# Moving parts of the float32r products at other byte offsets behind the weights, and a norm scratch of two lasting halves

## The chip, the cores and the metric

The kernel runs on one core of one Trainium2 chip. The metric is device time in microseconds, the median of the runs. The profile is of one further execution, taken by the hardware profiler. TensorE is called PE in its rows (PEld for its weight loads), VectorE DVE, ScalarE ACT, GpSimd POOL and SyncE SP.

## The reference

Two layers of a diffusion backbone over 256 latent tokens and 256 context tokens, width 1024, all in float32. Each layer is a feed-forward half block, a mixing stage with four branches, and a second feed-forward half block:

```python
for l in range(DEPTH):
    with_ctx_out = l < DEPTH - 1
    mod = jnp.split(jax.nn.silu(c) @ w_ada[l] + b_ada[l], N_MOD, axis=-1)     # likewise mod_c from c_ctx
    x = ffn_half(x, mod[0], mod[1], mod[2], ffn1_norm[l], ffn1_w_gate[l], ffn1_w_up[l], ffn1_w_down[l])
    h = ffn_half(h, mod_c[0], ...)                                            # the context tokens
    xn, hn = modulate(rmsnorm(x, mix_norm[l]), ...), modulate(rmsnorm(h, mix_norm[l]), ...)
    y, y_c = token_mixing(xn, hn, w_in[l], ..., w_branch[l], w_out[l], rope, with_ctx_out)
    x = x + mod[5] * y
    x = ffn_half(x, mod[6], mod[7], mod[8], ffn2_norm[l], ...)
    if with_ctx_out:
        h = h + mod_c[5] * y_c
        h = ffn_half(h, mod_c[6], mod_c[7], mod_c[8], ffn2_norm[l], ...)
return rmsnorm(x, final_norm)

def swiglu(z, wg, wu, wd):                 # in ffn_half, on the modulated norm of z
    return (jax.nn.silu(z @ wg) * (z @ wu)) @ wd
```

In the last layer the context tokens are needed only as keys and values, so behind its projections it works on 256 tokens, and all before that works on 512.

## The kernel before

**Products.** Features lie on the partitions and tokens along the free dimension, 512 columns for both kinds of tokens (the constant `TT`), 256 for the latent ones alone (`T`). Every large product is made of float32r products of split numbers: a weight is split into whi and wlo, a moving part into a high and a low half, and `mm3` issues three matmuls for each block of 128 features: whi with the high half (line 110), whi with the low half (line 111), wlo with the high half (line 112). Each matmul loads its 128 columns of weights, 512 bytes a partition, and streams 2048 bytes (512 columns) or 1024 bytes (256 columns) of the moving part.

**Stages.** For each layer: `ffn` (pg and pu are the gate and up products, with xs as the moving part; pd and last the down product, with hh and hl), `mix` (proj, gate and the other projections with xs; pb with bh and bl, the split branch outputs; po and last with mh and ml), `ffn` again. An `ffn` runs over two halves of 11 chunks; `first_units` does the first two chunks in blocks of 256 columns, in the very first block `cold_units` does them while the adaptive gains are still being computed (the cold start, up to 66.1 us). While it runs, `ada` sums the gains for later on VectorE and hands each set to PE in eight short matmuls (line 290). The second `ffn` of layer 1 works on 256 columns.

**Weights.** `unit` loads a weight tile (SP's queue), splits it on ScalarE (line 81) and VectorE (line 84), with four buffers of each, so that the tiles stand ready before PE needs them.

**Places.** xs is one long tile; `place` cuts xh and xl, the high and the low half of the normed input, out of it at offsets from the table `PLACES`. `hidden` cuts hh and hl out of padded tiles in the same way. Worked out from the sizes of the tiles in the order of their allocation, in bytes mod 512 (the weight tiles lie at 0; only those few that come from a feed-forward block's own pool lie at 256):

| moving parts | columns | before | after the change |
|---|---|---|---|
| xh, xl in layer 0 and the first `ffn` of layer 1 | 512 | 240, 368 | 368, 496 |
| hh, hl there | 512 | 112, 240 | 112, 496 |
| bh, bl in layer 0 | 512 | 0, 0 | 112, 240 or 368, 496 (two buffers) |
| mh, ml in layer 0 | 512 | 0, 0 | 0, 0 |
| xh, xl in the mixing stage and the second `ffn` of layer 1 | 256 (some 512) | 192, 192 | 448, 448 |
| hh, hl in the second `ffn` of layer 1 | 256 | 192, 192 | 448, 448 |
| bh, bl and mh, ml in layer 1 | 256 | 448, 448 | 448, 448 |

With the change the weights of the blocks' own pools lie at 0 as well, since the tile of hh grows by 256 bytes.

**The norm scratch.** `apply` makes the normed input of one segment (256 columns) for a list of blocks k: VectorE writes nt (line 368), ScalarE makes the high half of xs from it (line 371), VectorE the low half (line 372). nt is a tile of 512 columns with one buffer; each pair of blocks takes a new one and uses its two halves in turn. `cold_units` calls `apply` for a single k at a time, so there each call takes a new tile and uses its first half. The squares of `consts` (line 174) use the same buffer, and so does one tile of `score_parts` in the mixing stage.

**Order.** The order of the instructions on each engine is made by a planner that places every instruction when its operands and its buffer come free in its own model of the costs, earlier ones of the program first.

Of the kernel before, what the change touches and what calls it, by code (L numbers as in the profile page):

```python
# [10 lines left out]
F32 = mybir.dt.float32  # L11
F32R = mybir.dt.float32r
# [5 lines left out]
P = 128  # L18
L = 2
D = 1024  # L20
NK = D // P
T = 256
TT = 2 * T
# [22 lines left out]
LINE = 32  # L46


PLACES = {(0, C_N1): (28, NK * TT + LINE, (28, 12)), (0, C_NM): (28, NK * TT + LINE, None),
          (0, C_N2): (28, NK * TT + LINE, (28, 12)), (1, C_N1): (28, NK * TT + LINE, (28, 12)),  # L50
          (1, C_NM): (16, NK * TT + TT, None), (1, C_N2): (16, NK * TT + TT, (48, 0))}


def ada_chunks(s):
# [4 lines left out]
class Net:  # L59
# [76 lines left out]
    def consts(self):  # L136
        nc, cp, i = self.nc, self.cp, self.i
        self.x = cp.tile([P, NK, TT], F32, name="x")
        self.xs = cp.tile([P, 2 * NK * TT + TT + LINE], F32R, name="xs")
        self.cv = cp.tile([P, NK, 2], F32, name="cv")  # L140
        self.cols = [cp.tile([P, C_END], F32, name=f"cols{l}") for l in range(L)]
        self.mats = cp.tile([P, 3, P], F32, name="mats")
        self.ident, self.perm, self.bones = (self.mats[:, j] for j in range(3))
        for k in range(0, NK, 2):
            nc.sync.dma_start(self.x[:, k:k + 2], i["xT"][:, k:k + 2])
            if k == 0:
                nc.sync.dma_start(self.cv, i["cv"])
        nc.sync.dma_start(self.cols[0], i["cols"][0])
        self.eps = cp.tile([P, 1], F32, name="eps")
        nc.vector.memset(self.eps, EPS)  # L150
        self.junk = cp.tile([P, 1], F32, name="junk")
        self.warm(AF.Silu, self.eps)
        self.ones = cp.tile([P, P], F32, name="ones")
        nc.vector.memset(self.ones, 1.0)

        self.sil = cp.tile([P, NK, 32], F32, name="sil")
        nc.gpsimd.memset(self.sil, 0.0)
        nc.scalar.activation(self.sil[:, :, 0:2], self.cv, AF.Silu)

        self.pick = cp.tile([P, 32], F32, name="pick")  # L160
        nc.gpsimd.memset(self.pick, 0.0)
        for r in range(2):
            nc.gpsimd.memset(self.pick[64 * r:64 * r + 64, r:r + 1], 1.0)
        self.mod = [cp.tile([P, 72, 2], F32, name=f"mod{l}") for l in range(L)]
        self.have = [set() for _ in range(L)]

        ps = [self.aux("stat")[:, :T] for _ in range(2)]
        for k in range(NK):
            for r in range(2):
                sq = self.tp.tile([P, TT], F32, tag="nt", bufs=1, name="sq")[:, :T] if r else self.tp.tile(  # L170
                    [P, T], F32, tag="sq", name="sq")
                x = self.x[:, k, r * T:(r + 1) * T]
                if r:
                    nc.vector.tensor_tensor(out=sq, in0=x, in1=x, op=ALU.mult)
                else:
                    nc.scalar.activation(sq, x, AF.Square)
                nc.tensor.matmul(ps[r], self.ones, sq, start=k == 0, stop=k == NK - 1)
        self.rstd = {r: self.tp.tile([P, T], F32, tag="rstd", name="rstd") for r in range(2)}
        for r in range(2):
            nc.scalar.activation(self.rstd[r], ps[r], AF.Sqrt, scale=1.0 / D, bias=self.eps)  # L180
            nc.vector.reciprocal(self.rstd[r], self.rstd[r])

    def place(self, l, phase):

        h, d, o = PLACES[l, phase]
        self.xh, self.xl = (self.xs[:, a:a + NK * TT].rearrange("p (k t) -> p k t", t=TT) for a in (h, h + d))
        return o

    def keep_warm(self, n):

# [169 lines left out]
    def apply(self, g, sh, r, ks=range(NK)):  # L360

        nc = self.nc
        c0, c1 = HALF[r]
        for j, k in enumerate(ks):
            if j % 2 == 0:
                pair = self.tp.tile([P, TT], F32, tag="nt", bufs=1, name="nt")
            t = pair[:, j % 2 * T:j % 2 * T + T]
            nc.vector.scalar_tensor_tensor(out=t, in0=self.x[:, k, c0:c1], scalar=g[:, k, r:r + 1], in1=self.rstd[r],
                                           op0=ALU.mult, op1=ALU.mult)
            hi = self.xh[:, k, c0:c1]  # L370
            nc.scalar.activation(hi, t, AF.Identity, bias=sh[:, k, r:r + 1])
            nc.vector.scalar_tensor_tensor(out=self.xl[:, k, c0:c1], in0=t, scalar=sh[:, k, r:r + 1],
                                           in1=hi.bitcast(F32), op0=ALU.add, op1=ALU.subtract)
# [88 lines left out]
    def hidden(self, hp, off):  # L462

        return tuple(hp.tile([P, FH * TT + pad], F32R, tag=t, name=t)[:, a:a + FH * TT].rearrange(
            "p (f t) -> p f t", t=TT) for t, pad, a in zip(("hh", "hl"), (48, 16), off))

    def cold_units(self, wgu, hp, evac, off):

# [191 lines left out]
    def score_parts(self, pool, q, k, n, ks=None):  # L660


        nc = self.nc
        qs = [pool.tile([P, TT], F32R, tag=f"qs{h}", name="qs") for h in range(2)]
        ql = [pool.tile([P, TT], F32R, tag="ql", name="ql"), self.tp.tile([P, TT], F32R, tag="nt", bufs=1, name="ql")]
        for h in range(2):
            nc.gpsimd.memset(ql[h][64 - 64 * h:128 - 64 * h, :n].bitcast(F32), 0.0)
        new = ks is None
        if new:
            ks = [pool.tile([P, TT], F32R, tag=f"ks{h}", name="ks") for h in range(2)]  # L670
        for h in range(2):
            own, other = slice(64 * h, 64 * h + 64), slice(64 - 64 * h, 128 - 64 * h)
            nc.scalar.copy(qs[h][own, :n], q[own, :n])
            if new:
                nc.scalar.copy(ks[h][own], k[own])
            nc.scalar.copy(qs[h][other, :n], q[own, :n])
            if new:
                nc.vector.tensor_tensor(out=ks[h][other], in0=k[own], in1=ks[h][own].bitcast(F32), op=ALU.subtract)
            nc.vector.tensor_tensor(out=ql[h][own, :n], in0=q[own, :n], in1=qs[h][own, :n].bitcast(F32), op=ALU.subtract)
        return qs, ql, ks  # L680
# [156 lines left out]
    def mix(self, l, segs):  # L837
# [1 line left out]
        n = T * len(segs)  # L839
        ns = len(segs)  # L840
        cols = self.cols[l]
        self.place(l, C_NM)
        with tc.tile_pool(name=f"mix{l}", bufs=1) as mp:
            acc = mp.tile([P, NK, TT], F32, tag="macc", name="macc")
            if l == 0:
# [2 lines left out]
            def tmp(name, shape=(P, TT)):  # L848
                return bp.tile(list(shape), F32, tag="t", bufs=5, name=name)

            def branch():
                return (mp.tile([P, 2, TT], F32R, tag="bh", bufs=2, name="bh"),
                        mp.tile([P, 2, TT], F32R, tag="bl", bufs=2, name="bl"))

            def merge(b, bo, first=False):

# [388 lines left out]
```

## Time and profile before

| | us |
|---|---|
| median of 3 runs (2144.76 to 2150.27) | 2145.19 |
| the profiled execution | 2152.58 |
| its span, from the first to the last instruction | 2150.8 |
| PE busy in it | 2117.5 |
| DVE busy | 1440.8 |
| ACT busy | 904.6 |
| mean granted clock of PE, share of full | 0.996 |

The profiled execution is 0.3% longer than the median of the runs. "Busy" of PE covers overlapping matmuls: a row's duration runs from its start to its modelled end, and the next matmul starts before that end. The distance of two starts is what one of them costs in a stream.

### The profile page before, as it was taken

Reading aid. Unit: us, or ns where it says so; the run is one execution under the profiler, and the core shown is the slowest. Engines: PE = TensorE matmul, PEld = TensorE weight load, DVE = VectorE, ACT = ScalarE, POOL = GpSimd, SP = SyncE. Lnnn points to the kernel's source line nnn. Section 1 sums busy time; section 2 is a strip of 40 time slices with the busy share of each in tenths; the row PEclk is TensorE's granted clock in tenths of the full one; section 3 lists DMA queues with packets and bytes.
Section 4 is the critical chain, followed back from the end, with each engine's and each line's share of the span. In section 5 each row is a group of like instructions: output and inputs, shape, how many; then the busy total and the mean of one; then the engine's idle time right before and its main releaser. Section 6 shows DMA issues by size and latency. Waiting matters only on the chain.

```text
span 2150.8 us, 31652 instructions
## 1 busy us (share of the span) xinstructions
PE 2117.5 (98%) x12446; PEld 1809.5 (84%) x12446; DVE 1440.8 (67%) x2355; ACT 904.6 (42%) x1488; POOL 39.5 (2%) x95
## 2 busy tenths in 40 slices
PE   7999999999999999999999999999999999999998
PEld 5778778988888888888887888888789989999998
DVE  5987987676366455675676567657665867677555
ACT  3332333456546533433233243323234665656443
POOL 0000000001000000000000000000000000000000
PEclk9999999999999999999999999999999999999999
DMA  7645654321122122343454334445433232355553
GB/s 289 200 166 171 217 185 145 120 77 59 59 89 79 64 88 98 108 148 133 140 179 146 126 129 152 138 142 176 153 119 120 96 118 105 133 180 186 174 194 115
DMA packets 89509, 296.71 MB, mean 138 GB/s; under 512 B 10256, under 2 KB 12176, under 8 KB 89360
## 3 DMA queue, kind: packets, MB, share of 16 engines
q1 hardware_dynamic: 89360, 294.69, 40.7%
q8 instruction: 98, 1.61, 0.3%
q14 instruction: 51, 0.42, 0.1%
HBM read 293.60 MB, written 1.05 MB: 137 GB/s over the span
## 4 chain that ended last, share of the span: by engine, by line
PE 94%; DVE 3%; ACT 2%; issue 1%; DMA 0%; DVEq 0%; ACTq 0%; SPq 0%
PE pg L110 6%; PE pu L110 6%; PE pu L112 6%; PE pg L112 6%; PE pu L111 6%; PE pg L111 6%; PE pd L110 6%; PE pd L112 6%; PE pd L111 6%; PE gate L110 4%; PE gate L112 4%; PE gate L111 4%; PE proj L110 2%; PE proj L111 2%; PE proj L112 2%; PE blev L771 2%
## 5 line engine op out<-in xcount | busy, mean ns | idle before, releaser
L81 ACT CAST whi<-raw 128x1024 fp32r<-128x1024 f32 (+2 forms) x444 | 430.2, 971 | 881.6 <-PE pu L111 213.2
L84 DVE TENSOR_TENSOR wlo<-raw,whi 128x1024 fp32r<-128x1024 f32 (+2 forms) x444 | 498.5, 1124 | 311.4 <-ACT whi L81 308.5
L278 DVE SCALAR_TENSOR_TENSOR aacc<-araw,sil,aacc 128x512 f32<-128x512 f32 x448 | 313.1, 746 | 101.3 <-DMA araw<-in_wada 100.9
L110 PE MATMUL pg<-xs,whi 128*128 128x512 f32 (+1 forms) x640 | 238.0, 372 | 0.8 <-DVE sg L456 0.8
L110 PE MATMUL pu<-xs,whi 128*128 128x512 f32 (+1 forms) x640 | 237.9, 372 | 0.0
L111 PE MATMUL pu<-xs,whi 128*128 128x512 f32 (+1 forms) x640 | 235.1, 367 | 0.0
L111 PE MATMUL pg<-xs,whi 128*128 128x512 f32 (+1 forms) x640 | 235.1, 367 | 0.0
L112 PE MATMUL pg<-xs,wlo 128*128 128x512 f32 (+1 forms) x640 | 234.8, 367 | 0.0
L112 PE MATMUL pu<-xs,wlo 128*128 128x512 f32 (+1 forms) x640 | 234.8, 367 | 0.0
L112 PE MATMUL pd<-hh,wlo 128*128 128x512 f32 (+1 forms) x616 | 224.3, 364 | 0.0
L110 PE MATMUL pd<-hh,whi 128*128 128x512 f32 (+1 forms) x616 | 223.8, 363 | 0.0
L111 PE MATMUL pd<-hl,whi 128*128 128x512 f32 (+1 forms) x616 | 222.8, 362 | 0.0
L110 PE MATMUL gate<-xs,whi 128*128 128x512 f32 (+1 forms) x512 | 175.0, 342 | 0.0
L112 PE MATMUL gate<-xs,wlo 128*128 128x512 f32 (+1 forms) x512 | 173.0, 338 | 0.0
L111 PE MATMUL gate<-xs,whi 128*128 128x512 f32 (+1 forms) x512 | 172.2, 336 | 0.0
L110 PEld LDWEIGHTS pg<-xs,whi 128*128 128x128 f32 x640 | 120.9, 189 | 23.4 <-issue 2.0
L112 PEld LDWEIGHTS pu<-xs,wlo 128*128 128x128 f32 x640 | 121.4, 190 | 22.2
L112 PEld LDWEIGHTS pg<-xs,wlo 128*128 128x128 f32 x640 | 121.4, 190 | 22.2
L110 PEld LDWEIGHTS pu<-xs,whi 128*128 128x128 f32 x640 | 120.9, 189 | 22.3 <-issue 2.0
L111 PEld LDWEIGHTS pu<-xs,whi 128*128 128x128 f32 x640 | 121.2, 189 | 21.0
L111 PEld LDWEIGHTS pg<-xs,whi 128*128 128x128 f32 x640 | 121.2, 189 | 20.8
L110 PEld LDWEIGHTS pd<-hh,whi 128*128 128x128 f32 x616 | 116.3, 189 | 19.5 <-issue 2.2
(276 smaller groups left out, 3809.0 us busy)
## 6 DMA issues: line engine op xcount, KB each, us to landing
raw<-in_wgu SPq DMA_DIRECT2D x176, 512.0 KB, 3.4
araw<-in_wada SPq DMA_DIRECT2D x128, 512.0 KB, 3.2
raw<-in_wgate SPq DMA_DIRECT2D x64, 512.0 KB, 3.2
raw<-in_wd SPq DMA_DIRECT2D x64, 384.0 KB, 3.1
raw<-in_win SPq DMA_DIRECT2D x44, 512.0 KB, 3.2
raw<-in_wd SPq DMA_DIRECT2D x64, 320.0 KB, 2.8
aspace<-in_wada SPq DMA_DIRECT2D x16, 512.0 KB, 9.1
raw<-in_wbr SPq DMA_DIRECT2D x16, 512.0 KB, 3.4
```

The source lines that it names most:

```text
L81: nc.scalar.copy(hi, src)
L84: nc.vector.tensor_tensor(out=lo, in0=src, in1=hi.bitcast(F32), op=ALU.subtract)
L110: nc.tensor.matmul(ps, wh, a, start=first and j == 0, stop=False)
L111: nc.tensor.matmul(ps, wh, b, start=False, stop=False)
L112: nc.tensor.matmul(ps, wl, a, start=False, stop=last and j == n - 1)
L278: nc.vector.scalar_tensor_tensor(out=acc[r], in0=w[:, j], scalar=c, in1=acc[r], op0=ALU.mult, op1=ALU.add)
L771: nc.tensor.matmul(ps[:, g * P:(g + 1) * P], k[:, h, g * P:(g + 1) * P], x[:, h, (g ^ cross) * P:((g ^ cross) + 1) * P], start=True, stop= ...
```

## The change

xs gets 1536 bytes shorter (a multiple of 512, so that what lies behind it keeps its place mod 512), and `PLACES` gets other offsets for it; the tile of hh gets 256 bytes of padding more; the tiles of bh and bl are padded by 256 bytes each and cut at offsets that `PLACES` now gives for the mixing stage, one pair for each of the two buffers. `half` returns the two halves of one lasting nt tile in turn; the squares of `consts` and `apply` take their scratch from it, and `score_parts`, which allocates the same buffer for itself, makes it forget the tile.

```diff
--- before.py
+++ after.py
@@ -46,9 +46,9 @@
 LINE = 32
 
 
-PLACES = {(0, C_N1): (28, NK * TT + LINE, (28, 12)), (0, C_NM): (28, NK * TT + LINE, None),
-          (0, C_N2): (28, NK * TT + LINE, (28, 12)), (1, C_N1): (28, NK * TT + LINE, (28, 12)),
-          (1, C_NM): (16, NK * TT + TT, None), (1, C_N2): (16, NK * TT + TT, (48, 0))}
+PLACES = {(0, C_N1): (60, NK * TT + LINE, (28, 12)), (0, C_NM): (60, NK * TT + LINE, ((28, 60), (28, 60))),
+          (0, C_N2): (60, NK * TT + LINE, (28, 12)), (1, C_N1): (60, NK * TT + LINE, (28, 12)),
+          (1, C_NM): (80, NK * TT, ((0, 0), (64, 64))), (1, C_N2): (80, NK * TT, (112, 0))}
 
 
 def ada_chunks(s):
@@ -136,7 +136,8 @@
     def consts(self):
         nc, cp, i = self.nc, self.cp, self.i
         self.x = cp.tile([P, NK, TT], F32, name="x")
-        self.xs = cp.tile([P, 2 * NK * TT + TT + LINE], F32R, name="xs")
+        self.xs = cp.tile([P, 2 * NK * TT + 5 * LINE], F32R, name="xs")
+        self.nt = None
         self.cv = cp.tile([P, NK, 2], F32, name="cv")
         self.cols = [cp.tile([P, C_END], F32, name=f"cols{l}") for l in range(L)]
         self.mats = cp.tile([P, 3, P], F32, name="mats")
@@ -167,8 +168,7 @@
         ps = [self.aux("stat")[:, :T] for _ in range(2)]
         for k in range(NK):
             for r in range(2):
-                sq = self.tp.tile([P, TT], F32, tag="nt", bufs=1, name="sq")[:, :T] if r else self.tp.tile(
-                    [P, T], F32, tag="sq", name="sq")
+                sq = self.half() if r else self.tp.tile([P, T], F32, tag="sq", name="sq")
                 x = self.x[:, k, r * T:(r + 1) * T]
                 if r:
                     nc.vector.tensor_tensor(out=sq, in0=x, in1=x, op=ALU.mult)
@@ -185,6 +185,13 @@
         h, d, o = PLACES[l, phase]
         self.xh, self.xl = (self.xs[:, a:a + NK * TT].rearrange("p (k t) -> p k t", t=TT) for a in (h, h + d))
         return o
+
+    def half(self):
+
+        if self.nt is None:
+            self.nt, self.nth = self.tp.tile([P, TT], F32, tag="nt", bufs=1, name="nt"), T
+        self.nth = T - self.nth
+        return self.nt[:, self.nth:self.nth + T]
 
     def keep_warm(self, n):
 
@@ -361,10 +368,8 @@
 
         nc = self.nc
         c0, c1 = HALF[r]
-        for j, k in enumerate(ks):
-            if j % 2 == 0:
-                pair = self.tp.tile([P, TT], F32, tag="nt", bufs=1, name="nt")
-            t = pair[:, j % 2 * T:j % 2 * T + T]
+        for k in ks:
+            t = self.half()
             nc.vector.scalar_tensor_tensor(out=t, in0=self.x[:, k, c0:c1], scalar=g[:, k, r:r + 1], in1=self.rstd[r],
                                            op0=ALU.mult, op1=ALU.mult)
             hi = self.xh[:, k, c0:c1]
@@ -462,7 +467,7 @@
     def hidden(self, hp, off):
 
         return tuple(hp.tile([P, FH * TT + pad], F32R, tag=t, name=t)[:, a:a + FH * TT].rearrange(
-            "p (f t) -> p f t", t=TT) for t, pad, a in zip(("hh", "hl"), (48, 16), off))
+            "p (f t) -> p f t", t=TT) for t, pad, a in zip(("hh", "hl"), (112, 16), off))
 
     def cold_units(self, wgu, hp, evac, off):
 
@@ -663,6 +668,7 @@
         nc = self.nc
         qs = [pool.tile([P, TT], F32R, tag=f"qs{h}", name="qs") for h in range(2)]
         ql = [pool.tile([P, TT], F32R, tag="ql", name="ql"), self.tp.tile([P, TT], F32R, tag="nt", bufs=1, name="ql")]
+        self.nt = None
         for h in range(2):
             nc.gpsimd.memset(ql[h][64 - 64 * h:128 - 64 * h, :n].bitcast(F32), 0.0)
         new = ks is None
@@ -839,7 +845,7 @@
         n = T * len(segs)
         ns = len(segs)
         cols = self.cols[l]
-        self.place(l, C_NM)
+        off = self.place(l, C_NM)
         with tc.tile_pool(name=f"mix{l}", bufs=1) as mp:
             acc = mp.tile([P, NK, TT], F32, tag="macc", name="macc")
             if l == 0:
@@ -848,9 +854,13 @@
             def tmp(name, shape=(P, TT)):
                 return bp.tile(list(shape), F32, tag="t", bufs=5, name=name)
 
+            turn = 1
+
             def branch():
-                return (mp.tile([P, 2, TT], F32R, tag="bh", bufs=2, name="bh"),
-                        mp.tile([P, 2, TT], F32R, tag="bl", bufs=2, name="bl"))
+                nonlocal turn
+                turn = 1 - turn
+                pair = [mp.tile([P, 2 * TT + 2 * LINE], F32R, tag=t, bufs=2, name=t) for t in ("bh", "bl")]
+                return tuple(t[:, a:a + 2 * TT].rearrange("p (c t) -> p c t", t=TT) for t, a in zip(pair, off[turn]))
 
             def merge(b, bo, first=False):
```

## Rows read from the trace of the kernel before

**Rows 1.** The page: busy time of each engine, and the chain by engine.

```profile
PE 2117.5 (98%) x12446; PEld 1809.5 (84%) x12446; DVE 1440.8 (67%) x2355; ACT 904.6 (42%) x1488; POOL 39.5 (2%) x95
...
PE 94%; DVE 3%; ACT 2%; issue 1%; DMA 0%; DVEq 0%; ACTq 0%; SPq 0%
```

**Rows 2.** Groups by line and shape, PE: busy us, mean ns of one.

```profile
L110 PE MATMUL pg<-xs,whi 128*128 128x512 f32 x480 | 192.9, 402 | 0.0
...
L111 PE MATMUL pg<-xs,whi 128*128 128x512 f32 x480 | 190.1, 396 | 0.0
L112 PE MATMUL pg<-xs,wlo 128*128 128x512 f32 x480 | 189.9, 396 | 0.0
...
L112 PE MATMUL pd<-hh,wlo 128*128 128x512 f32 x462 | 181.0, 392 | 0.0
L110 PE MATMUL pd<-hh,whi 128*128 128x512 f32 x462 | 180.5, 391 | 0.0
L111 PE MATMUL pd<-hl,whi 128*128 128x512 f32 x462 | 179.5, 389 | 0.0
```

**Rows 3.** Timeline of PE, pg: start us, us, instruction; 17 rows lie between.

```profile
100.86 0.40 PE L110 MATMUL pg<-xs,whi 128*128 128x512 f32 x1
...
105.08 0.40 PE L110 MATMUL pg<-xs,whi 128*128 128x512 f32 x1
```

**Rows 4.** Timeline of PE, pd; 59 rows lie between.

```profile
184.85 0.39 PE L110 MATMUL pd<-hh,whi 128*128 128x512 f32 x1
...
198.45 0.39 PE L110 MATMUL pd<-hh,whi 128*128 128x512 f32 x1
```

**Rows 5.** Timeline of PE, gate and pb: 23 rows lie between, then 5.

```profile
812.74 0.40 PE L110 MATMUL gate<-xs,whi 128*128 128x512 f32 x1
...
818.29 0.39 PE L110 MATMUL pb<-bh,whi 128*128 128x512 f32 x1
...
819.65 0.40 PE L110 MATMUL gate<-xs,whi 128*128 128x512 f32 x1
```

**Rows 6.** Timeline of PE behind the cold units: 16 triples, then 7.

```profile
66.11 0.40 PE L110 MATMUL pg<-xs,whi 128*128 128x512 f32 x1
...
77.20 0.40 PE L110 MATMUL pg<-xs,whi 128*128 128x512 f32 x1
...
82.06 0.40 PE L110 MATMUL pg<-xs,whi 128*128 128x512 f32 x1
```

**Rows 7.** Timeline of PE, layer 1, 256 columns, gate: six triples, then two.

```profile
1722.17 0.28 PE L110 MATMUL gate<-xs,whi 128*128 128x256 f32 x1
...
1724.21 0.28 PE L110 MATMUL pb<-bh,whi 128*128 128x256 f32 x1
...
1724.89 1.05 PE L771 MATMUL blev<-bqz,bk 128*128 128x128 f32 x8
```

**Rows 8.** Timeline of PE, layer 1, last block: eight triples, then eight.

```profile
1967.66 0.28 PE L110 MATMUL pu<-xs,whi 128*128 128x256 f32 x1
...
1970.49 0.28 PE L110 MATMUL pg<-xs,whi 128*128 128x256 f32 x1
...
1973.31 0.28 PE L110 MATMUL pu<-xs,whi 128*128 128x256 f32 x1
```

**Rows 9.** The cold start: PE's waits, timeline, and one stretch by engine.

```profile
PE mm L123 <- ACT xs L371: 8.2, 3, 5.1
...
53.66 0.48 DVE L368 SCALAR_TENSOR_TENSOR nt<-x,gain,rstd 128x256 f32<-128x256 f32 x1
...
56.91 0.48 DVE L368 SCALAR_TENSOR_TENSOR nt<-x,gain,rstd 128x256 f32<-128x256 f32 x1
...
57.98 0.79 PE L123 MATMUL mm<-xs,whi 128*128 128x512 f32 x1 [5.14 <-ACT xs L371]
...
57.00:66.10 9.10, 8.12 (x24) 6.44 (x25) 8.94 (x16) 4.13 (x7) 0.00 (x0) 0.65 0.50 167
```

**Rows 10.** Stretches by engine: length, PE, PEld, DVE, ACT, POOL busy, clock, DMA.

```profile
66.10:169.00 102.90, 102.90 (x464) 81.85 (x463) 86.97 (x132) 35.34 (x48) 0.00 (x0) 1.00 0.54 181
```

## The prediction

> **What bounds the kernel now.** I read the page first: TensorE is busy for 98% of the span, and 94% of the chain of work that ended last is TensorE [rows 1]. Then the groups by line with their shapes, and then the timeline of TensorE alone, because "busy" there says little: the matmuls overlap, so what counts is the distance from one start to the next. Each product of this kernel is a triple on lines 110, 111 and 112 (high weights with high moving part, high weights with low moving part, low weights with high moving part), so I take the distance from one L110 row to the next as the price of a triple. Nothing waits in these stretches; the triples run back to back, and yet they don't all cost the same:
>
> - pg of the first feed-forward block, 512 columns: six triples in 105.08 - 100.86 = 4.22 us, 0.703 us each [rows 3].
> - pd of the same block, 512 columns, same kind of weights, same function: twenty triples in 198.45 - 184.85 = 13.60 us, 0.680 us each [rows 4].
> - gate and pb in a stretch of the mixing stage without side work, 512 columns: eight gate triples in 5.55 us, 0.694 each, and the two pb triples right behind them in 1.36 us, 0.680 each [rows 5].
>
> The last one is the telling one. gate and pb alternate in one stream on one engine, through the same function, with the same weight tiles; what differs is where the moving parts lie (240 and 368 bytes behind the weights, mod 512, for gate; 0 and 0 for pb). pd has 112 and 240. So a triple of 512 columns has at least two prices, 0.680 and about 0.70, and the place of the moving part goes with them. The means of one matmul say the same: 402 + 396 + 396 = 1194 ns for pg and 391 + 389 + 392 = 1172 ns for pd, 22 ns a triple [rows 2].
>
> **The change part by part.**
>
> *xh and xl for 512 columns.* Their places go from (240, 368) to (368, 496), all mod 512; mod 256 that is from (240, 112) to (112, 240), which is where pd has its parts. Does a place count mod 256 or mod 512? In the first chunk behind the cold units the weights come from the block's own pool and lie at 256, so that xh and xl are at (496, 112) there; the chunk behind it has (240, 368). The sixteen triples of the first take 77.20 - 66.11 = 11.09 us, 0.693 each, and seven of the second take 4.86 us, 0.694 each [rows 6]. A shift by 256 changes nothing measurable, so I take (368, 496) as equal to (112, 240), and the price as pd's.
> The three feed-forward blocks that run 512 columns have 20 chunks with 8 triples of pg and 8 of pu in each, 3 x 20 x 16 = 960 triples. I take the 22 ns of the means [rows 2] and not the 23 ns of the undisturbed stretches [rows 3, 4], since the means hold the interruptions by the ada matmuls: 960 x 22 ns = 21.1 us. gate in layer 0 has 4 x 8 x 8 = 256 triples, proj with 512 columns in layer 0 has 15 x 8 = 120. Both are broken up by side work, so I take only the quiet difference of 13.5 ns [rows 5]: 376 x 13.5 ns = 5.1 us. Sum 26.2 us. All of it lies on TensorE, which sets the end; bounds: nothing, if the price goes with something else than the place, and 1336 x 23 ns = 30.7 us, if every triple gains the full step.
>
> *hh, hl, bh, bl.* hh and hl keep (112, 240) mod 256: the tile of hh grows by 256 bytes, so hl and the pool's own weights move by 256, and the weights there come to lie at 0 like all others. bh and bl go from (0, 0) to (112, 240), from 0.680 [rows 5] to 0.680 [rows 4]: nothing. mh and ml stay.
>
> *256 columns, layer 1.* xs and hh/hl go from 192 to 448. Here too there are two prices: 0.340 us a triple (six gate triples in 2.04 us) and 0.353 (eight pu triples in 2.83 us) [rows 7, 8]. But place does not tell them apart. gate at 192 runs at 0.340 and pb at 448 right behind it too, (1724.89 - 1724.21) / 2 = 0.340 [rows 7]; pu at 448 (weights of the block's pool, at 256) runs at 0.353 and pg at 192 right behind it too, 2.82 us for eight [rows 8]. A stream keeps the price with which it began. So I take nothing for this part. Its bounds: the 496 triples of the second feed-forward block (pg 160, pu 160, pd 154, last 22) and the gate and proj triples (328) could all fall to the low price, 824 x 13.3 ns = 11.0 us less, though part of gate is there already [rows 7]; or gate and proj could all go to the high one, at most 328 x 13.3 ns = 4.4 us more.
>
> *The norm scratch.* Until now a call of apply for one k takes a new nt tile with one buffer, so the next call can't write until both readers of the last one are done. With two halves of a lasting tile it can write while ScalarE still reads. The place where this binds is the cold start, where apply is called for single k: TensorE waited there three times, 8.2 us in all, for ScalarE's xs, once for 5.1 us [rows 9]. In that case the nt of the first half ran at 53.66, 0.48 long, and that of the other half only at 56.91, 2.8 us later than it could; the matmul that needs both began at 57.98. The order on VectorE is the planner's, and once the second nt is free to run it should stand right behind the first. I take 2.8 us for this wait, 1.2 us for the two smaller ones, 4.0 us together. [...] The work that nt overtakes (a wlo, an aacc) belongs to weights that are used only behind 66.1, so it costs nothing.
>
> *What is late next.* With TensorE 3% faster in the feed-forward blocks VectorE must keep up: it is busy for 86.97 of 102.90 us in the densest stretch, with the ada sums in it [rows 10]; 22 ns on 1194 make that 85% to 86%. It stays hidden.
>
> [...]
>
> **How the numbers follow.** Sum: 26.2 + 4.0 = 30.2 us. The durations are of the profiled execution, 2152.6 us with a span of 2150.8; the median of the runs is 2145.2, 0.3% below. The steps are steps of a locked stream, so I take them off the median as they are: 2145.2 - 30.2 = 2115.
>
> **The rivals.**
> - *B, layer 1 falls to the low price as well.* For it: which price a stream keeps is settled where it begins, and all beginnings move; against it: 448 shows both prices. If the second feed-forward block goes over as one stream, 496 x 13.3 ns = 6.6 us, and some of gate with it, 2 us: 2106. Chance 0.30.
> - *C, the place is worth nothing* or the change misses its place, and only the scratch counts: the price would go with, say, the PSUM bank or the side engines' work. For it: pg and pd differ in more than the place. Against it: gate and pb [rows 5]. 2145.2 - 4.0 = 2141. Chance 0.08.
> - *D, slower.* Places count mod 512 after all, and (368, 496) is worse than what is there. The place is every 512-column triple on xs: if all of them settle at 0.71 us (an estimate, a little above the 0.703 of [rows 3]), the 960 lose 7 ns (6.7 us) and the 376 lose 16 ns (6.0 us); with the 4.4 us of layer 1 that is 17 us, less the 4.0 of the scratch: 2158. It decides for slower from about 0.705 us a triple on. Against it: [rows 6]. Chance 0.04.
> - *E, half.* xs settles between 0.680 and 0.694, because the last steps of the lock depend on more than the two places: about 13 us less, 2128. Chance 0.08.
> The forecast itself, A, has 0.50.
>
> The range: A's own terms reach from 2145.2 - 30.7 - 10.7 = 2104 to 2145.2 - 21.1 + 4.4 = 2128. B lies in it but for its lower part; with B I let it begin at 2101. E's middle is its upper end. Left out are C, D and the outer parts of B and E, together about 0.2. A measurement of this kernel can tell about 0.3% from no change, 6.4 us: A, B and E are faster by more (0.88), C lies within (0.08), D is slower (0.04).
>
> **What would show each step.** Right, if L110 rows of pg and gate with 512 columns come 0.680 us apart, the mean of the three pg rows falls from 1194 to about 1172 ns, and those of pd stay; wrong, if pg stays at 0.70. The scratch: TensorE's wait for xs on L123 falls from 8.2 to about 4 us, with nt rows in pairs before 66 us, and the first pg row comes 4 us earlier than 66.11. Layer 1: pg and pu of the last block still 0.353 us a triple; 0.340 is B. What would make it all wrong: a plan that sets the work of the mixing stage in another order, with new waits there; idle time of TensorE in that stage would show it.

## The result, and the profile after

The kernel after takes 2115.5 us (median of 2109.65, 2115.50, 2115.57 and 2115.61), the kernel before 2147.7 us in the runs beside it (2144.76 to 2151.32). The ratio is 0.984, with an interval of 0.982 to 0.987. The profiled execution of after took 2115.61 us with a span of 2113.8 us; that of before took 2152.58 us with 2150.8 us.

One thing has to be known to read any of these times. The runs of nearly every kernel here fall into two groups some 6 us apart: before at 2143 to 2147 and 2150 to 2153, after near 2109.6 and near 2115.5. It is one stretch that makes them, the second feed-forward block of layer 1, the last block of the kernel, whose 496 triples of 256 columns run at 0.340 us each in some executions and at 0.353 in others. 496 x 13.3 ns = 6.6 us. In the eight profiled executions of kernels whose runs fall into two such groups, price and group go together every time. Both profiled executions, of before and of after, are of the upper group, so they can be compared as they stand; of the medians, after's lies in the upper group, before's 2147.7 between the two, and the 2145.2 from which the prediction started in the lower one.

The page of after: busy time by engine, and the chain that ended last, by engine. TensorE is still 94% of that chain [rows 1].

```profile
PE 2087.5 (99%) x12446; PEld 1801.0 (85%) x12446; DVE 1434.9 (68%) x2355; ACT 904.5 (43%) x1488; POOL 39.4 (2%) x95
...
PE 94%; DVE 2%; ACT 2%; issue 1%; DMA 0%; DVEq 0%; ACTq 0%; SPq 0%
```

The groups by line and shape of after, TensorE (busy us, mean ns of one). The three matmuls of a pg triple have gone from 402 + 396 + 396 to 391 + 388 + 392 ns; those of pd stand where they were [rows 2].

```profile
L112 PE MATMUL pg<-xs,wlo 128*128 128x512 f32 x480 | 188.1, 392 | 0.0
L110 PE MATMUL pg<-xs,whi 128*128 128x512 f32 x480 | 187.5, 391 | 0.0
L111 PE MATMUL pg<-xs,whi 128*128 128x512 f32 x480 | 186.4, 388 | 0.0
L112 PE MATMUL pd<-hh,wlo 128*128 128x512 f32 x462 | 181.0, 392 | 0.0
L110 PE MATMUL pd<-hh,whi 128*128 128x512 f32 x462 | 180.5, 391 | 0.0
L111 PE MATMUL pd<-hl,whi 128*128 128x512 f32 x462 | 179.4, 388 | 0.0
```

The timeline of after, start and length in us. First VectorE in the cold start: nt now comes in pairs, where before its two halves lay 3.25 us apart [rows 9]. Then the first pg triple behind the cold units, then seven triples of pg, and at the end the last block.

```profile
47.58 0.88 DVE L373 SCALAR_TENSOR_TENSOR nt<-x,gain,rstd 128x256 f32<-128x256 f32 x2
50.31 0.87 DVE L373 SCALAR_TENSOR_TENSOR nt<-x,gain,rstd 128x256 f32<-128x256 f32 x2
...
55.00 0.39 PE L110 MATMUL pg<-xs,whi 128*128 128x512 f32 x1
...
88.28 0.39 PE L110 MATMUL pg<-xs,whi 128*128 128x512 f32 x1
...
93.04 0.39 PE L110 MATMUL pg<-xs,whi 128*128 128x512 f32 x1
...
1927.28 0.36 PE L110 MATMUL pg<-xs,whi 128*128 128x256 f32 x1 [0.44 <-ACT xs L376]
...
1935.83 0.28 PE L110 MATMUL pu<-xs,whi 128*128 128x256 f32 x1
...
1938.66 0.28 PE L110 MATMUL pg<-xs,whi 128*128 128x256 f32 x1
...
1941.49 0.28 PE L110 MATMUL pu<-xs,whi 128*128 128x256 f32 x1
```

Seven pg triples take 93.04 - 88.28 = 4.76 us, 0.680 each, against 0.703 before [rows 3]. The first pg row comes at 55.00 and not at 66.11 [rows 6]. In the last block eight pu triples take 2.83 us and the eight pg triples behind them too: 0.353, as before [rows 8].

The waits of TensorE in the first 70 us, and the stretch ahead of the first pg row (length, then busy time of PE, PEld, DVE, ACT and POOL, granted clock, DMA share, GB/s). Where before lost 8.2 us to three waits for xs and ran the stretch behind the longest of them at a clock of 0.65 [rows 9], after loses 2.6 us, and the stretch ahead of its first pg row is at 1.00.

```profile
PE mm L123 <- ACT xs L376: 2.6, 3, 0.9
```

```profile
49.00:55.00 6.00, 5.91 (x25) 4.51 (x25) 6.00 (x12) 4.23 (x7) 0.00 (x0) 1.00 0.25 87
```

So the two profiled executions divide cleanly at the first pg row. Up to it: 66.11 - 55.00 = 11.1 us gained. From it to the end: (2150.8 - 66.1) - (2113.8 - 55.0) = 25.9 us. Together 37.0 us (group against group the runs give 35; the profiled execution of before lies at the top of its group). The prediction had 4.0 and 26.2.

### The profile page after: what moved, and what is told of

It reads as the page before. It is cut to its first block, busy times and chain, and to the rows that moved or that the text cites. A ratio compares the mean times of both kernels' runs of the same rounds, so it can differ in the third digit from the quotient of the medians.

```text
span 2113.8 us, 31650 instructions
## 1 busy us (share of the span) xinstructions
PE 2087.5 (99%) x12446; PEld 1801.0 (85%) x12446; DVE 1434.9 (68%) x2355; ACT 904.5 (43%) x1488; POOL 39.4 (2%) x95
## 4 chain that ended last, share of the span: by engine, by line
PE 94%; DVE 2%; ACT 2%; issue 1%; DMA 0%; DVEq 0%; ACTq 0%; SPq 0%
PE pg L110 6%; PE pu L110 6%; PE pg L112 6%; PE pu L112 6%; PE pg L111 6%; PE pu L111 6%; PE pd L110 6%; PE pd L112 6%; PE pd L111 6%; PE gate L112 4%; PE gate L110 4%; PE gate L111 4%; PE proj L111 2%; PE proj L110 2%; PE proj L112 2%; PE blev L777 2%
## 5 line engine op out<-in xcount | busy, mean ns | idle before, releaser
L110 PE MATMUL pg<-xs,whi 128*128 128x512 f32 (+1 forms) x640 | 232.5, 363 | 0.4 <-ACT xs L376 0.4
L110 PE MATMUL pu<-xs,whi 128*128 128x512 f32 (+1 forms) x640 | 232.3, 363 | 0.0
L111 PE MATMUL pg<-xs,whi 128*128 128x512 f32 (+1 forms) x640 | 231.4, 362 | 0.0
L111 PE MATMUL pu<-xs,whi 128*128 128x512 f32 (+1 forms) x640 | 231.3, 361 | 0.0
L110 PE MATMUL pd<-hh,whi 128*128 128x512 f32 (+1 forms) x616 | 223.8, 363 | 0.0
L110 PE MATMUL gate<-xs,whi 128*128 128x512 f32 (+1 forms) x512 | 172.5, 337 | 0.0
L110 PEld LDWEIGHTS pg<-xs,whi 128*128 128x128 f32 x640 | 120.8, 189 | 20.8 <-issue 1.8
L110 PEld LDWEIGHTS pu<-xs,whi 128*128 128x128 f32 x640 | 120.8, 189 | 20.1 <-issue 2.0
L111 PEld LDWEIGHTS pu<-xs,whi 128*128 128x128 f32 x640 | 120.2, 188 | 19.4
L111 PEld LDWEIGHTS pg<-xs,whi 128*128 128x128 f32 x640 | 120.2, 188 | 19.4
L110 PEld LDWEIGHTS pd<-hh,whi 128*128 128x128 f32 x616 | 116.2, 189 | 19.5 <-issue 2.2
```

The source lines that it names most:

```text
L110: nc.tensor.matmul(ps, wh, a, start=first and j == 0, stop=False)
L111: nc.tensor.matmul(ps, wh, b, start=False, stop=False)
```

## The experiments

Two theories were to be told apart first. **The place theory**, that of the prediction: a triple's price goes with where its two moving parts lie relative to the weights, mod 256. **The rival**: the price goes with something else that pd has and pg has not, and most of the gain comes from the cold start. After the first runs a second question was added: what sets the price of the last block.

### The place alone

```
 (the change, but in consts and apply the scratch as before:)
-            t = self.half()
+            if j % 2 == 0:
+                pair = self.tp.tile([P, TT], F32, tag="nt", bufs=1, name="nt")
+            t = pair[:, j % 2 * T:j % 2 * T + T]
...
```

> The new places with the norm scratch of before. Theory 1 (places and scratch are two separate gains, places as in the sum, scratch larger than the sum said): 25 to 26 us less than before, pg triples of 512 columns at 0.680 us, first pg row still near 66.1 us. Theory 2 (the places gained more than the trace of after shows, through what comes later): 30 us less or more. Theory 3 (they help each other, the places alone are worth less): 20 us less or fewer.

Measured: 2120.4 us (2119.5 to 2121.0), ratio 0.988 (0.986 to 0.990). Its last block runs at 0.340, so it stands beside the lower group of before (2143.8 to 2145.9 in these runs): 24.5 us. Its first pg row comes at 66.16, as before. Groups of this run by line and shape; 277 and 276 ns are a block at 0.340; before and after, profiled at 0.353, have 281 to 282 ns in these rows:

```profile
L110 PE MATMUL pg<-xs,whi 128*128 128x256 f32 x160 | 44.2, 277 | 0.8 <-DVE sg L464 0.8
L110 PE MATMUL pu<-xs,whi 128*128 128x256 f32 x160 | 44.2, 276 | 0.0
```

Added up over the timeline, from each L110 row to the next, the triples of pg and pu with 512 columns are 19.4 us shorter in the kernel after than in the one before (716 to 695 ns on average, interruptions included), those of gate 3.9 us and those of proj 1.9 us: 25.2 us, within 1 us of what this run shows.

### The scratch alone

```
 (the kernel before, with the scratch of the change:)
-            t = pair[:, j % 2 * T:j % 2 * T + T]
+            t = self.half()
...
-                sq = self.tp.tile([P, TT], F32, tag="nt", bufs=1, name="sq")[:, :T] if r else ...
+                sq = self.half() if r else ...
```

> The places of before with the two lasting halves. Theory 1: 10 to 11 us less than before, first pg row near 55 us, TensorE's wait for xs on L123 near 2.6 us and no half clock between 46 and 66 us. Theory of the sum on record: 4 us less, first pg row near 62 us. Theory 3: nearly nothing, since the matmuls of the cold start at the old places would take up what the scratch frees.

Measured: 2137.6 us, runs of 2133.6 to 2135.0 and of 2140.2 to 2141.0, 10.7 and 11.0 us below the two groups of before (the upper one has only two runs there); ratio 0.996 (0.994 to 0.998). The rows of this run that answer to [rows 9], from the waits, the timeline and the stretches:

```profile
PE mm L123 <- ACT xs L376: 2.6, 3, 0.9
```

```profile
55.75 0.40 PE L110 MATMUL pg<-xs,whi 128*128 128x512 f32 x1
```

```profile
26.00:32.00 6.00, 5.97 (x78) 3.53 (x76) 2.54 (x8) 0.09 (x1) 0.00 (x0) 1.00 1.02 415
```

The first pg row is 10.4 us earlier than in the kernel before, and the clock is 1.00 in every six-microsecond stretch from 20 us up to it, where before had 0.73 in the one shown here. 24.5 + 10.7 = 35.2 us: place and scratch add up to the whole change, and the rival's "most of it is the cold start" falls.

### The scratch, part by part

The sum of the prediction had 4 us for the scratch and named apply alone. Two runs divide it. Halves in apply, and one fixed place for the squares of the first statistic:

```
 (the kernel before, with half() in apply, and in consts:)
+                    self.half()
+                    sq = self.nt[:, :T]
...
```

> The kernel before, with the two halves of the scratch used by apply alone; the squares of the first statistic keep one place, so that each waits for the reader of the last. If apply's wait is the whole of the gain: the first pg row comes at about 55.8, as with both, and the time is 10 to 11 us below the kernel before. If the squares carry a part: the statistic is finished at 17.4 as before (14.7 with both), the first pg row comes at about 58 to 59, and the gain is about 8 us. By the sum of the prediction it would be 4 us.

Halves for the squares, and apply as before:

```
 (the kernel before, and in consts:)
+                sq = self.half() if r else self.tp.tile([P, T], F32, tag="sq", name="sq")
...
```

> The kernel before, with the two halves used by the squares of the first statistic alone; apply keeps its pair with one buffer. If the squares matter by themselves: the statistic is finished 2.7 us earlier and the first pg row comes about 2.7 us earlier than 66.11, so that the time falls by 2 to 3 us. If the later waits for apply take that up: the first pg row stays at 65 to 66 and the time within 1 us of the kernel before.

Measured, apply alone: 2143.1 us, and here the groups matter: eleven of its twelve runs lie at 2142.4 to 2144.9 and one at 2136.6, against 2150.7 to 2152.9 and 2143.5 to 2146.3 for before in the runs beside it, so some 9 us on either level, though the ratio of the medians says 0.998 (0.996 to 0.999). Squares alone: 2148.0 us, ratio 1.001 (1.000 to 1.002, which doesn't exclude no change); but its groups, 2145.8 to 2148.3 and 2153.2 to 2155.4, lie on average 2.1 and 2.5 us above those of before. First the timeline of apply alone:

```profile
57.03 0.39 PE L110 MATMUL pg<-xs,whi 128*128 128x512 f32 x1
```

Then the waits, the timeline and two stretches of squares alone:

```profile
PE mm L123 <- ACT xs L378: 8.3, 5, 5.1
```

```profile
68.48 0.40 PE L110 MATMUL pg<-xs,whi 128*128 128x512 f32 x1
```

```profile
20.00:26.00 6.00, 2.79 (x15) 2.01 (x13) 5.91 (x10) 2.90 (x4) 0.00 (x0) 0.85 1.02 415
26.00:32.00 6.00, 6.00 (x50) 3.06 (x49) 1.45 (x3) 1.01 (x2) 0.00 (x0) 0.58 0.52 187
```

Apply carries 66.1 - 57.0 = 9.1 us of it, somewhat more than the 8 us expected if the squares carry a part. The squares bring the statistic forward (its last matmul on L177 starts at 14.55 and not at 16.67), and by themselves that is a loss: the first pg row comes 2.4 us later. TensorE then stands idle in 20 to 26 us, first for a DMA and then for xs (busy for 2.79 us, before 3.04), the waits for xs are as long as ever (8.3 us in all, before 8.2 [rows 9]), and in the next stretch the clock is at 0.58 where before had 0.73. With apply's halves on top, the earlier statistic is worth another 57.0 - 55.75 = 1.3 us by these two executions, and some 2 us by the groups (10.7 and 11.0 against 9); the seven profiled executions that have the whole change in their cold start put the first pg row anywhere from 54.5 to 55.4, so the size of this part is known only roughly. The parts don't add (9.1 - 2.4 is not 10.4); neither of my two expectations for the squares had a loss. That the clock makes the loss is read from the stretches and not shown: the plan sets the short matmuls of the cold start in another order too, and no run held the clock or the order fixed.

### The low and the high part exchanged

```
-PLACES = {(0, C_N1): (60, NK * TT + LINE, (28, 12)), ...
+PLACES = {(0, C_N1): (60, NK * TT + LINE, (60, 44)), ...
...
-            "p (f t) -> p f t", t=TT) for t, pad, a in zip(("hh", "hl"), (112, 16), off))
+            "p (f t) -> p f t", t=TT) for t, pad, a in zip(("hh", "hl"), (112, 144), off))
```

> The kernel after, with the hidden parts hh and hl of the three feed-forward blocks of 512 columns swapped from (112, 240) to (240, 112) bytes behind the weights, mod 256; all else the same, pg and pu keep (112, 240). If the place sets the price: the L110 rows of pd go from 0.680 to about 0.700 us apart (the sweep behind the kernel showed 0.703 for (240, 112)), pg stays at 0.680, and the time rises by 3 x 154 = 462 triples x about 20 ns = 9 us, to about 2119 or 2125 (with the last block at 0.340 or at 0.353). If the price goes with something else of pd (its loop, its weights, its bank): pd stays at 0.680 and the time at 2110 or 2116.

Measured: 2117.9 and 2118.5, 2124.8 and 2125.0 us, 8.5 us above the lower group of after and 9.3 above the upper. Groups by line and shape of this run:

```profile
L110 PE MATMUL pg<-xs,whi 128*128 128x512 f32 x480 | 187.5, 391 | 0.0
...
L110 PE MATMUL pd<-hh,whi 128*128 128x512 f32 x462 | 185.5, 401 | 0.0
L112 PE MATMUL pd<-hh,wlo 128*128 128x512 f32 x462 | 182.7, 395 | 0.0
L111 PE MATMUL pd<-hl,whi 128*128 128x512 f32 x462 | 182.5, 395 | 0.0
```

pd has taken over nearly the price that pg had before, 401 + 395 + 395 = 1191 ns against 1171 in after (pg before: 1194), and 462 x 20 ns = 9.2 us is the time. Nothing of pd was touched but the place. The place theory stands, and gate against pb [rows 5], on which the prediction rested, was read rightly.

### A sweep of places

Behind the kernel after, streams of triples with each place in turn, each begun behind one small float32 matmul (two for the last quarter):

```
+            for d in range(0, 256, 16):
+                stream(d, d, TT, 2, 1)
+            for d in range(0, 256, 16):
+                stream(d, (d + 128) % 512, TT, 2, 1)
+            for kick in (1, 2):
+                for d in range(0, 512, 32):
+                    stream(d, d, T, 3, kick)
```

> The kernel after, and behind its output streams of triples on copied data that nothing reads: 512 columns with high and low part both d bytes behind the weights, d = 0, 16 to 240; then the low part 128 bytes behind the high one; then 256 columns with both at d = 0, 32 to 480, twice, behind one and behind two short float32 products. Some 540 us more than after. If the place sets the price: (112, 240) 0.680 us a triple, (240, 112) 0.693 or 0.703, (192, 192) 0.700, (0, 0) 0.680 or 0.691, and a shift by 256 changes nothing at 256 columns either: d and d + 256 alike, 192 and 448 at 0.340 or 0.353, 0 and 256 at 0.360. If the price belongs to the stages and not to the places: one price for all d.

Timeline of this run, L1112 the small matmuls (one counts as x2), L1120 the first of each triple: 512 columns at (112, 240), 512 columns at (240, 112) mod 256, then 256 columns at 192 behind one small matmul, and behind two.

```profile
2372.35 0.39 PE L1120 MATMUL sweep<-mv,sw 128*128 128x512 f32 x1
...
2381.19 0.39 PE L1120 MATMUL sweep<-mv,sw 128*128 128x512 f32 x1
...
2462.82 0.40 PE L1120 MATMUL sweep<-mv,sw 128*128 128x512 f32 x1
...
2471.96 0.40 PE L1120 MATMUL sweep<-mv,sw 128*128 128x512 f32 x1
...
2525.16 0.38 PE L1112 MATMUL kick<-swf 128*128 128x128 f32 x2
...
2525.73 0.28 PE L1120 MATMUL sweep<-mv,sw 128*128 128x256 f32 x1
...
2533.51 0.28 PE L1120 MATMUL sweep<-mv,sw 128*128 128x256 f32 x1
...
2666.45 0.61 PE L1112 MATMUL kick<-swf 128*128 128x128 f32 x4
...
2667.25 0.29 PE L1120 MATMUL sweep<-mv,sw 128*128 128x256 f32 x1
...
2674.74 0.28 PE L1120 MATMUL sweep<-mv,sw 128*128 128x256 f32 x1
```

13 triples in 8.84 us are 0.680 at (112, 240); 13 in 9.14 us are 0.703 at (240, 112), the prices of [rows 4] and [rows 3] with nothing beside them. At 192, 22 triples take 7.78 us behind one small matmul and 7.49 us behind two: 0.353 and 0.340, one place, two prices, and what differs is the number of small matmuls ahead of the stream. The other streams, by the same reading of the timeline (mean us of a triple):

| columns | places (high, low), mod 512 | behind one | behind two |
| --- | --- | --- | --- |
| 512 | (0, 0) / (112, 240) | 0.680 / 0.680 | |
| 512 | (64, 64), (144, 272) | 0.687, 0.686 | |
| 512 | (112, 112) / (0, 128) | 0.693 / 0.693 | |
| 512 | (192, 192) / (160, 288) / (240, 240) | 0.700 / 0.707 / 0.709 | |
| 256 | 0 and 256 | 0.360, 0.360 | 0.360, 0.359 |
| 256 | 32 and 288 | 0.350, 0.350 | 0.350, 0.350 |
| 256 | 192 and 448 | 0.353, 0.353 | 0.341, 0.341 |

A place and the same place 256 bytes on have the same price to within 0.4 ns in all eight pairs and both ways of beginning. For layer 1, which the change moves from 192 to 448, it therefore does nothing.

### Layer 1 back at 192

```
-          (1, C_NM): (80, NK * TT, ((0, 0), (64, 64))), (1, C_N2): (80, NK * TT, (112, 0))}
+          (1, C_NM): (16, NK * TT, ((0, 0), (64, 64))), (1, C_N2): (16, NK * TT, (48, 64))}
...
-            "p (f t) -> p f t", t=TT) for t, pad, a in zip(("hh", "hl"), (112, 16), off))
+            "p (f t) -> p f t", t=TT) for t, pad, a in zip(("hh", "hl"), (112, 144), off))
```

> The kernel after, with xs and the hidden parts of layer 1 back at 192 instead of 448 (mod 512). If 192 and 448 are alike for 256 columns: the time of after, on one of its two levels (near 2115.6 or near 2109.7), pg and pu of the last block at 0.353 or 0.340 us a triple throughout. If 448 is the better place: slower by 2 us or more on each level, and gate and proj of layer 1 at 0.353 us more often.

Measured: 2108.55 and 2108.56, 2115.2 and 2116.4 us, the two groups of after within 1.1 us. In the kernel, as in the sweep, 448 is 192.

### All pairs of places for 256 columns, and the kernel at the best one

If the last block's price hangs on how its stream begins, is there a place where it doesn't? A second sweep took 16 x 16 pairs, behind one small matmul and behind two:

```
+            for kick in (1, 2):
+                for d in range(0, 256, 16):
+                    for e in range(0, 256, 16):
+                        stream(d, e, T, 2, kick)
```

> The kernel after, with streams of 16 triples of 256 columns behind it, one for each of 16 x 16 pairs of places (high part, low part; steps of 16 bytes, mod 256), each begun behind one or behind two small float32 matmuls. The earlier sweep, with both parts at one place, showed 192 at 0.340 or 0.353 by how the stream began, and all others at 0.350 to 0.360 whichever way. If 0.340 belongs to that one place: of the 512 streams only (192, 192) behind two shows it. If it belongs to a set of pairs, as 0.680 does for 512 columns ((112, 240), (0, 0)): some pairs show 0.340 behind one and behind two alike, and such a pair would hold the last feed-forward block at 0.340, worth 496 x 13.3 ns = 6.6 us where the kernel after runs it at 0.353. The work behind the kernel adds about 3000 us, which say nothing of the kernel.

Of the 512 streams three end at 0.340: (192, 192) behind two, and (112, 112) both ways. All others lie between 0.347 and 0.367. That the price goes with the way of beginning isn't special to (192, 192): at 43 of the 256 pairs the two ways end more than 2.5 ns apart. The timeline of (112, 112), behind one and behind two; ten triples take 3.40 us both times:

```profile
2805.59 0.39 PE L1112 MATMUL kick<-swf 128*128 128x128 f32 x2
...
2807.58 0.28 PE L1120 MATMUL sweep<-mv,sw 128*128 128x256 f32 x1
...
2810.98 0.28 PE L1120 MATMUL sweep<-mv,sw 128*128 128x256 f32 x1
...
4341.96 0.61 PE L1112 MATMUL kick<-swf 128*128 128x128 f32 x4
...
4344.17 0.28 PE L1120 MATMUL sweep<-mv,sw 128*128 128x256 f32 x1
...
4347.57 0.28 PE L1120 MATMUL sweep<-mv,sw 128*128 128x256 f32 x1
```

So the kernel after with layer 1 at (112, 112), and beside it, on the same chip, the kernel after itself:

```
-          (1, C_NM): (80, NK * TT, ((0, 0), (64, 64))), (1, C_N2): (80, NK * TT, (112, 0))}
+          (1, C_NM): (60, NK * TT, ((44, 44), (44, 44))), (1, C_N2): (60, NK * TT, (92, 44))}
...
-            "p (f t) -> p f t", t=TT) for t, pad, a in zip(("hh", "hl"), (112, 16), off))
+            "p (f t) -> p f t", t=TT) for t, pad, a in zip(("hh", "hl"), (112, 144), off))
```

> The kernel after, with the parts of layer 1 that are read with 256 columns (xs, hh and hl, bh and bl) moved from (192, 192) to (112, 112) bytes behind the weights, mod 256: the only pair of the sweep of 16 x 16 pairs that showed 0.340 us a triple behind one small matmul and behind two. If the sweep holds in the kernel: the last feed-forward block runs at 0.340 in every run (its stage about 186 us, not 193), the gate and pb triples of layer 1 that still run at 0.353 (128 and 29) go to 0.340 too, another 157 x 13.3 ns = 2 us, and all runs lie in one group at about 2107. If the price of the stream is settled by what runs ahead of it and not by the place: two groups as before, about 2109 and 2115.

> The kernel after itself, on the same chip and beside the same runs of the kernel before, so that the level of its runs is known better than from four. Two groups, near 2109.6 and 2115.6, as the last block runs at 0.340 or at 0.353; like for like 35 us below the two groups of the kernel before (2145 and 2151).

Measured: 2107.2 us (2106.1 to 2107.6, one group), ratio to before 0.981 (0.980 to 0.983); the kernel after beside it 2115.4 us (2115.0 to 2116.2, this time all in the upper group, 36 us below the two upper runs of before), ratio 0.985 (0.984 to 0.987). The timeline of the last block at (112, 112), from its first triple:

```profile
1925.73 0.36 PE L110 MATMUL pg<-xs,whi 128*128 128x256 f32 x1 [0.43 <-ACT xs L376]
1926.16 0.28 PE L110 MATMUL pg<-xs,whi 128*128 128x256 f32 x1
...
1927.23 0.28 PE L110 MATMUL pg<-xs,whi 128*128 128x256 f32 x1
...
1936.75 0.28 PE L110 MATMUL pg<-xs,whi 128*128 128x256 f32 x1
...
1939.47 0.28 PE L110 MATMUL pu<-xs,whi 128*128 128x256 f32 x1
```

The stream begins as it does in after, behind a wait for ScalarE, its first triples cost 0.357 (three in 1.07 us), and then it falls to 0.340 (eight in 2.72 us) and stays (275 to 276 ns is the mean of each pg and pu row of the block, where after has 281). It is the fastest version here, 38 us below before by the medians, and its five runs show no second group; that no execution would fall into one, five runs can't show.

## Why the prediction came out as it did

**The price of a place: right, and shown.** pg at 0.680, pd unmoved, the mean of three pg rows at 1171 ns (1172 foretold), and pd made dearer at will by the exchange: with weights, order and columns the same, it moved pd by 20 ns a triple through 128 bytes of place. Of the terms, xs was 21.1 us and measured 19.4, gate with proj 5.1 and measured 5.8: 26.2 against 25.2. The step of 22 ns had been taken from means of durations; the distances of the starts shrank by 20 ns. Rivals C and E are out, and D's premise, that places count mod 512, is refuted: pg at (368, 496) has the price of pd at (112, 240), 0.680 us, and in the sweep 256 columns cost the same 256 bytes on, to within 0.4 ns. One thing stays open: all weights lie at 0 mod 256 before and after, so no run tells a place relative to the weights from a place in itself.

**Mod 256: right, and it decided more than was seen.** The sixteen triples of [rows 6] showed that 256 bytes change nothing (0.693 us against 0.694); the same argument says that 192 and 448 are one place, so that layer 1's edit can't do anything at all. The prediction took nothing for it, but kept bounds of -11.0 and +4.4 us and a chance of 0.30 for rival B. The exchange of 192 and 448, with both groups within 1.1 us, shows that the edit has no part in it.

**The scratch: the term that was mis-sized.** 4.0 us were summed, and the range took off 10.7 us for it at most. No run shows that 10.7 as a limit; in its place the runs showed 10.7 us (the scratch alone) to 11.1 us (in after). The stretches up to the first pg row, of before and of after, in the columns used above:

```profile
0.00:66.11 66.11, 49.42 (x401) 35.03 (x401) 39.71 (x80) 23.32 (x40) 1.93 (x9) 0.92 0.74 268
```

```profile
0.00:55.00 55.00, 45.18 (x401) 32.49 (x401) 32.28 (x70) 22.31 (x39) 1.84 (x9) 1.00 0.77 292
```

With the same 401 matmuls, TensorE's idle time falls from 16.7 to 9.8 us, and its busy time from 49.4 to 45.2: 6.9 + 4.2 = 11.1. The waits for xs give 5.6 us of the idle time, where 4.0 were summed. The two smaller ones gave 1.3 (1.2 foretold), but the longest fell by 4.35 (5.14 to 0.79) and not by 2.8. The second nt was priced rightly there; what was missed is that the first one moves as well: before has a wlo and two aacc on VectorE between the transposition of the sums and the first nt, which starts 2.35 us behind it (51.31 to 53.66), and after has it 0.81 us behind (46.77 to 47.58). The other 1.2 us of idle time are small waits that the sum didn't have. And the clock, put at nothing in the sum, did come back: where before had 0.65 behind its longest wait [rows 9], no microsecond of the cold start of after is below 1.00, and the 96 large matmuls of the cold units, each counted to its end or the next start, take 25.1 us where before took 28.1 (the scratch alone, at the old places, 25.2). So the steps that failed are the price of the longest wait and the clock behind it. The squares, which the diff changes too, were not priced at all; with apply's halves they were worth 1.3 us more by the traces, alone -2.4.

The scratch had an effect on "What is late next" too. The first feed-forward stretch of after, in the same columns:

```profile
55.00:156.00 101.00, 101.00 (x468) 81.91 (x467) 92.91 (x144) 36.57 (x50) 0.00 (x0) 1.00 0.62 203
```

VectorE is busy for 92% of it and not for the 85% to 86% foretold. It stays hidden, for TensorE waits for nothing there, but its reserve is about half of what the prediction had: work that before did ahead of its first pg row now falls behind it. With the place alone, from the first pg row to the first pd row, the share is 87%, and with the scratch alone 90%.

**The base: an error that hid the other.** "I take them off the median as they are" set 30.2 us against 2145.2, a median of the lower group, and the runs of after lie mostly in the upper one. Group against group the change is worth 35 us (2145 to 2109.6, 2151 to 2115.5); by the same steps rightly sized the forecast would have been 2110 or 2116. That 2115 was met within 0.5 us is luck: it is owed to some 7 us too little for the scratch and 6 us of a block that happened to run at 0.353. The sign stood on the page: the profiled execution of before lay 7.4 us above the median, its last block ran at 0.353 [rows 8], and rival B's price for that very block was 6.6 us. Those two numbers belonged together.

**What hid rival B.** "A stream keeps the price with which it began" was right once its first two or three triples are past, and the sweep shows it by itself (22 triples in a row at 0.353, or at 0.340); but the conclusion, that all beginnings move and so B may come, missed that the beginning differs from one execution to the next, in the kernel before too. What differs there stays open. It is not the length of the wait ahead of the block: that is 0.81 us in before, at 0.353, and in squares alone, at 0.340, and 0.44 us in after, at 0.353, and in layer 1 back at 192, at 0.340. The first pg row of the last block in before, in squares alone and in layer 1 back at 192:

```profile
1964.76 0.36 PE L110 MATMUL pg<-xs,whi 128*128 128x256 f32 x1 [0.81 <-DVE sg L456]
```

```profile
1966.85 0.36 PE L110 MATMUL pg<-xs,whi 128*128 128x256 f32 x1 [0.81 <-DVE sg L463]
```

```profile
1927.22 0.36 PE L110 MATMUL pg<-xs,whi 128*128 128x256 f32 x1 [0.44 <-ACT xs L376]
```

What in the chip holds a stream at its price, no run here shows.

## What to carry to other kernels

Where a stream on one engine runs without waits and similar instructions still have two prices (here 0.680 and 0.703 us a triple), look at addresses before anything else: a sweep of a few hundred short streams behind the kernel gave the whole table in one profile, and the best entry could be put straight in. Before predicting, ask why the profiled execution and the median of the runs differ, and find the stretch that makes the difference; a base on the wrong level costs as much as a term. And where a long wait is followed by a lower granted clock (here 0.65 behind 5.1 us), put the slower work behind it into the sum, and ask which other instructions will move when one scratch comes free.

## What was not expected of the hardware

- In the sweeps a triple of float32r matmuls with 512 columns cost from 0.680 to 0.709 us by the places of its moving parts mod 256, the weights at 0; with 256 columns from 0.340 to 0.367. The order matters: (112, 240) was 0.680, (240, 112) 0.703.
- The best place was not the same for the two widths: in the first sweep (0, 0) was among the best at 512 columns (0.680) and among the worst at 256 (0.360).
- At (192, 192) two prices are stable, 0.340 and 0.353 us, through nearly all the 496 triples of a block (pg, pu and pd rows of 276 to 277 ns in layer 1 back at 192, of 281 to 282 in before); of the 256 pairs swept only (112, 112) settled at 0.340 behind one small matmul and behind two.
- Making an operand earlier can go with a longer time: with the earlier statistic alone TensorE was idle a little longer ahead of the cold units (busy for 2.79 of 6 us, before 3.04), the granted clock behind it was 0.58 (before 0.73), and the kernel some 2 us slower. That the one makes the other is not shown.
